# Two heads of a pair side by side on the halves of the matmul array

## Chip, core and metric

The kernel runs on one core of one Trainium2 chip. The metric is the device time of one execution in microseconds (us); less is better. TensorE (PE in the profile) does matmuls and transposes into PSUM, a small memory of eight banks per partition; VectorE (DVE), ScalarE (ACT) and GpSimd (POOL) do the elementwise work; SyncE (SP) issues the transfers. The array of TensorE is 128 rows (the contracted dimension) by 128 columns (the output partitions). A matmul whose contracted dimension is 64 uses one half of its rows, one whose output has 64 partitions one half of its columns; in the profile these have the forms 64\*128 and 128\*64.

## What is computed

An encoder of two layers on 1024 tokens of width 1024. Each layer projects x into the inputs of three groups, joins their outputs by one output projection, adds the residual and normalises, and then runs a gated feed-forward network with a second residual and norm. The groups are a gated linear recurrence, a retention with six heads of 64, and neighbourhood attention with four heads of 64 on a grid of 16 rows by 64 columns. Cut to the two groups at hand:

```
# retention, per head and chunk of 128 tokens
s = (q_chunk @ k_chunk.T) * decay          # 128 x 128
o = s @ v_chunk + (terms carried over the chunks), then a norm per head

# neighbourhood attention, per head: query (row, column) sees 8 x 16 keys
s = q @ k.T / 8 + bias(head, row distance, column distance)
p = softmax(s);  o = p @ v
```

## The kernel before

Activations are kept transposed (features on partitions, tokens along the free dimension). Heads come in pairs: a tile of 128 partitions holds head 0 in partitions 0 to 63 and head 1 in 64 to 127. Matmul operands of the large products are split into a high and a low part (`hi`, `lo`, type fp32r) and multiplied in three passes; the transposes and the products of attention values are plain fp32, where one matmul of the program appears as two instructions in the trace.

**Order of the work.** A layer is written as lists of steps that `weave` merges by their share of each list's cost, so that matmul-heavy steps (projections, output projection) stand between steps of the mixing groups. Below it the framework's list scheduler makes each engine's order at compile time: of what is ready it takes what stands first in the program, and it fills what it takes for a wait with later work. `order` fixes the order of two instructions of one engine. Buffers come from pools with tags: PSUM has `mm` (2 banks), `mx` (3, by `px_`), `mo` (1) and `ml` (2); SBUF has `T` (18 tiles of 4 KB per partition), `S` (8 of 2 KB), `Q` (4 of 2 KB) and others.

**Neighbourhood attention** (`na_mix`, L653) handles a pair of heads. A tile is 128 queries (8 rows by 16 columns: half `hf` of the rows, column block `cb`) of one head against 384 keys. Before, 16 tiles per pair run in the order head, half, column block, and a layer has two pairs, so 64 tiles in all. `scores` does two matmuls into one `mx` bank: the first contracts 128 rows (`nka` or `nkb`, which hold the high part of the keys in both halves, against the high and the low part of the head's queries), the second 64 rows (`nl`, the low part of the keys, in the head's own half). Then DVE adds the bias table and takes the maximum (L672), ACT makes the exponential and its sum (L675), DVE scales (L677). `values`, two tiles later in the list, transposes the three blocks of 128 keys into an `mx` bank (L691), ACT copies them (L693), and three fp32 matmuls of the form 128\*64 (six instructions) accumulate into the head's 64 partitions of `no`, the one `mo` bank. After the fourth column block ACT copies 64 partitions to `yna` (L702).

**Tables.** `na_table` (L636) builds the bias table of one head and half: one `T` tile (`tab`) and one `Q` tile (`tabc`), two POOL memsets (L641) and 16 transfers (L649, L650). Column blocks 0 to 2 read `tab`, block 3 reads `tabc`. With the head outermost, the query and key tiles of head 0 (`nqa`, `nka`) are last read half-way through a pair.

**What stands beside it.** The list of the layer's neighbourhood attention is woven with the projections of the second pair and the first half of the output projection (`wo`, tiles `res` of tag `T`), in one stage of about 126 us per layer.

**Retention** (`ret_mix`, `half`): per pair and half of the sequence, `scores` computes for each head four matmuls of the form 64\*128 into an `mx` bank, first all of head 0, then all of head 1, and DVE multiplies by the decay (L529). There are twelve such steps (two layers, three pairs, two halves), each of 16 instructions in the trace. The matmuls of `outs` (`o`) and of `kv` already alternate between the heads; those of `kv` are of the form 128\*64, as the values of neighbourhood attention are.

Of the kernel before, what the change touches and what calls it, by code (L numbers as in the profile page):

```python
# [11 lines left out]
AF = mybir.ActivationFunctionType  # L12
ALU = mybir.AluOpType
# [3 lines left out]
P = 128  # L17
# [13 lines left out]
TYPES = (0, 1, 1, 2)  # L31
# [21 lines left out]
class Trunk:  # L53
# [400 lines left out]
    def ret_mix(self, pr, z, ys):  # L454
        nc, l, V, A, G = self.nc, self.l, self.nc.vector, self.nc.scalar, self.nc.gpsimd
        blk = lambda t, w: t.rearrange("p (n i) -> p n i", i=w)
# [49 lines left out]
        def half(n4):  # L506
            sl = slice(n4 * 512, n4 * 512 + 512)
            w = {}

            def cross():  # L510
                w["qd"] = []
                for h in range(2):
                    hp = slice(h * 64, h * 64 + 64)
                    t = self.S("qd")
                    for d in range(2):
                        self.mark = G.tensor_tensor(out=blk(t, P)[d * 64 : d * 64 + 64, :, :], in0=blk(z["rq"][hp, sl], P),
                                                    in1=self.qw[hp, pr : pr + 1, d, :].to_broadcast([64, 4, P]), op=ALU.mult)
                    w["qd"].append(t)

            def scores():  # L520
                w["sd"] = []
                for h in range(2):
                    s = self.px_("s")
                    hp = slice(h * 64, h * 64 + 64)
                    for n in range(4):
                        c = (n4 * 4 + n) * P
                        self.mm(s[:, n * P : (n + 1) * P], z["rk"][hp, c : c + P], z["rq"][hp, c : c + P], True, True)
                    t = self.S("sd")
                    V.tensor_tensor(out=blk(t, P), in0=blk(s, P),  # L529
                                    in1=self.decay[:, 2 * pr + h : 2 * pr + h + 1, :].to_broadcast([P, 4, P]), op=ALU.mult)  # L530
                    w["sd"].append(t)

            def outs():
                o = self.px_("o")
                last = None
                for n in range(4):
                    m = n4 * 4 + n
                    c = slice(n * P, (n + 1) * P)
                    ks = slice(64 if m == 0 else 0, 64 if m == 7 else P)
                    ops = []  # L540
                    for h in range(2):
                        hp = slice(h * 64, h * 64 + 64)
                        ops.append((o[hp, c], z["st"][ks, m, hp], w["qd"][h][ks, c]))
                    for h in range(2):
                        hp = slice(h * 64, h * 64 + 64)
                        ops.append((o[hp, c], self.vc[pr][:, m, hp], w["sd"][h][:, c]))
                    for i, (out, lh, rh) in enumerate(ops):
                        ins = self.mm(out, lh, rh, i < 2, i >= 2)
                        if last is not None:
                            self.order(ins, last)  # L550
                        last = ins
                sq, sh, so = w["sd"][0], self.S("sqh", F32R), self.S("sql", F32R)
                A.activation(sh, o, AF.Square)
                A.activation(sq, o, AF.Square)
                self.lo(so, sq, sh)
                w["o"], w["sq"], w["sh"], w["sl"] = o, sq, sh, so

            def gnorm():
                sq = w["sq"]
                pv = self.px_("var")  # L560
                self.mm(pv, self.bones, w["sh"], True, False)
                self.mm(pv, self.bones, w["sl"], False, True)
                A.activation(sq, pv, AF.Ln, bias=self.gneps)
                A.activation(sq, sq, AF.Exp, scale=-0.5)
                V.tensor_tensor(out=sq, in0=w["o"], in1=sq, op=ALU.mult)
                V.scalar_tensor_tensor(out=ys[3 + pr][:, sl], in0=sq, scalar=self.gnw[:, l, pr : pr + 1], in1=z["sg"][:, sl],
                                       op0=ALU.mult, op1=ALU.mult)

            return [cross, scores, outs, gnorm]

        def spill():
# [79 lines left out]
        return tab[:, 0, :], tab[:, 1, :], tabc  # L651

    def na_mix(self, pr, z, ys):  # L653
        nc, V, A = self.nc, self.nc.vector, self.nc.scalar
        w = {}

        def scores(h, hf, cb):
            def step():
                if h == 0 and hf == 0 and cb == 0:
                    ys[6 + pr] = self.T("yna")  # L660
                if cb == 0:
                    w["tab"] = self.na_table(2 * pr + h, hf)
                grid = lambda t: t.rearrange("p (r c) -> p r c", c=64)
                hp = slice(h * 64, h * 64 + 64)
                s = self.px_("ns")
                c0 = COLS[cb]
                for i, (kp, b) in enumerate(((slice(0, P), z["nk"][h]), (hp, z["nl"]))):
                    self.mm(s[:, :384], z["nq"][h][kp, hf * 512 + cb * P : hf * 512 + cb * P + P],
                            grid(b)[kp, hf * 4 : hf * 4 + 12, c0 : c0 + 32], i == 0, i == 1)
                p = self.S("np")  # L670
                mx, sm = self.M("mx", 1), self.M("sm", 1)
                V.tensor_tensor_reduce(out=p[:, :384], in0=s[:, :384], in1=w["tab"][TYPES[cb]], scale=1.0,  # L672
                                       scalar=-3.0e38, op0=ALU.add, op1=ALU.max, accum_out=mx)
                V.tensor_scalar(mx, mx, -1.0, None, op0=ALU.mult)
                A.activation(p[:, :384], p[:, :384], AF.Exp, bias=mx, accum_out=sm)  # L675
                V.reciprocal(sm, sm)
                V.tensor_scalar(p[:, :384], p[:, :384], sm, None, op0=ALU.mult)  # L677
                w[h, hf, cb] = p

            return step  # L680

        def values(h, hf, cb):
            def step():
                hp = slice(h * 64, h * 64 + 64)
                if cb == 0:
                    w["o"] = self.ps("no", "mo")
                    w["last"] = None
                o, p = w["o"], w[h, hf, cb]
                pt = self.px_("npt")
                for g in range(3):  # L690
                    nc.tensor.transpose(pt[:, g * P : (g + 1) * P], p[:, g * P : (g + 1) * P], self.ident)  # L691
                pT = self.S("npT")
                A.activation(pT[:, :384], pt[:, :384], AF.Copy)  # L693
                for g in range(3):
                    gg = hf + g
                    ins = self.mm(o[hp, cb * P : (cb + 1) * P], self.vwin[gg][:, cb, (2 * pr + h) * 64 : (2 * pr + h) * 64 + 64],
                                  pT[:, g * P : (g + 1) * P], g == 0, g == 2)
                    if w["last"] is not None:
                        self.order(ins, w["last"])
                    w["last"] = ins  # L700
                if cb == 3:
                    A.activation(  # L702
                        ys[6 + pr][hp, hf * 512 : hf * 512 + 512].rearrange("p (r b c) -> p b r c", b=4, c=16)[:, :, :, ::-1],
                        o[hp, :].rearrange("p (b r c) -> p b r c", b=4, c=16), AF.Copy,
                    )

            return step

        tiles = [(h, hf, cb) for h in range(2) for hf in range(2) for cb in range(4)]
        steps = []  # L710
        for i in range(len(tiles) + 2):
            if i < len(tiles):
                steps.append(scores(*tiles[i]))
            if i >= 2:
                steps.append(values(*tiles[i - 2]))
        return steps


# [692 lines left out]
```

## Time and profile before

| | |
|---|---|
| time, median of 3 runs | 2349.53 us (2345.99 to 2353.46) |
| the profiled execution | 2347.68 us, span 2345.9 us |
| mean granted TensorE clock | 0.988 |
| TensorE busy | 2274.2 us, 97% |
| VectorE, ScalarE, GpSimd busy | 62%, 42%, 39% |

The span runs from the first to the last instruction. A matmul's shown duration includes its way through the array, so the durations of neighbours overlap; what a matmul costs TensorE is read from its start to the start of the next. PEld rows are loads of the stationary operand.

### The profile page before, as it was taken

The numbers are of one execution on the slowest core, as the hardware profiler recorded it, in microseconds if no ns is written. First come the engines' busy times: TensorE is split into PE (matmuls) and PEld (weight loads), VectorE is DVE, ScalarE is ACT, GpSimd is POOL, SyncE is SP. The second block draws the span as 40 slices with busy tenths as digits, with TensorE's granted clock in tenths as the row PEclk, the third lists the DMA queues.
The fourth block names the chain that finished last, engine by engine and source line by source line (L and its number), as shares of the span: only waits on it lengthen the run. The fifth ranks groups of instructions, "written<-read, shape, count | busy, mean of one in ns | idle before, by whom it ended". The sixth has DMA issues, their size and how long they took to land. (4 is left out here: it accounts for less than half of the span.)

```text
span 2345.9 us, 29309 instructions
## 1 busy us (share of the span) xinstructions
PE 2274.2 (97%) x10790; PEld 1834.5 (78%) x10790; DVE 1451.3 (62%) x2073; ACT 990.4 (42%) x1509; POOL 925.6 (39%) x568
## 2 busy tenths in 40 slices
PE   8999999999899999999989999999998999999998
PEld 6787777787678888888778878777876788888886
DVE  6966635578675656543658656455886656655336
ACT  5653345444233333443346533553542233344432
POOL 1424500054554343375513245000545543434655
PEclk9999999999999999999999999999999999999999
DMA  5232233424554445785321322333245444467852
GB/s 171 99 113 64 64 118 90 134 91 141 188 182 155 156 162 183 291 293 182 123 72 46 114 63 67 116 100 123 95 157 187 163 166 145 169 203 291 287 158 85
DMA packets 142696, 340.45 MB, mean 145 GB/s; under 512 B 24024, under 2 KB 37336, under 8 KB 142552
## 3 DMA queue, kind: packets, MB, share of 16 engines
q1 hardware_dynamic: 142552, 338.58, 43.7%
q8 instruction: 84, 1.38, 0.2%
q14 instruction: 60, 0.49, 0.1%
HBM read 242.88 MB, written 90.08 MB: 142 GB/s over the span
## 5 line engine op out<-in xcount | busy, mean ns | idle before, releaser
L116 PE MATMUL dn<-dw,hx 128*128 128x512 f32 x1848 | 422.0, 390 | 2.0 <-DVE rs L735 2.0
L116 PEld LDWEIGHTS dn<-dw,hx 128*128 128x128 f32 x1848 | 347.7, 188 | 74.5 <-DVE dw L122 2.4
L122 POOL TENSOR_TENSOR hx<-hraw,hx 128x1024 fp32r<-128x1024 f32 x80 | 207.7, 2611 | 195.3 <-ACT hx L119 188.5
L119 ACT ACTIVATE wsp<-qS 128x512 fp32r<-128x512 f32 x176 | 110.7, 631 | 277.5 <-PE w_up L116 134.6
L122 DVE TENSOR_TENSOR dw<-wraw,dw 128x1024 fp32r<-128x1024 f32 x84 | 124.4, 1488 | 158.0 <-ACT dw L119 147.8
L122 DVE TENSOR_TENSOR wsp<-qS,wsp 128x512 fp32r<-128x512 f32 x176 | 164.3, 935 | 62.9 <-ACT wsp L119 61.2
L119 ACT ACTIVATE dw<-wraw 128x1024 fp32r<-128x1024 f32 x84 | 83.1, 989 | 202.9 <-PE dn L116 187.3
L122 DVE TENSOR_TENSOR wl<-wraw,wh 128x1024 fp32r<-128x1024 f32 (+2 forms) x84 | 110.6, 1327 | 74.2 <-ACT wh L119 67.7
L119 ACT ACTIVATE wh<-wraw 128x1024 fp32r<-128x1024 f32 (+2 forms) x84 | 84.5, 1014 | 120.1 <-PE rg L116 27.6
L896 POOL TENSOR_TENSOR qS<-wraw 128x512 f32<-128x512 f32 x44 | 72.3, 1643 | 144.8 <-DVE wsp L122 75.1
L122 DVE TENSOR_TENSOR wsp<-wraw,wsp 128x512 fp32r<-128x512 f32 x100 | 114.4, 1147 | 23.8 <-ACT wsp L119 22.9
L119 ACT ACTIVATE wsp<-wraw 128x512 fp32r<-128x512 f32 x100 | 62.7, 629 | 130.5 <-PE w_up L116 76.4
L116 PE MATMUL wo<-wh,yh 128*128 128x512 f32 x256 | 104.1, 407 | 0.0
L116 PE MATMUL wo<-wl,yh 128*128 128x512 f32 x256 | 101.9, 398 | 0.0
L116 PE MATMUL wo<-wh,yl 128*128 128x512 f32 x256 | 100.9, 394 | 0.0
L1029 DVE TENSOR_TENSOR w_gate<-w_gate,w_gate 128x512 f32<-128x512 f32 x58 | 39.7, 684 | 90.2 <-PE w_gate L116 60.3
L119 ACT ACTIVATE hx<-hraw 128x1024 fp32r<-128x1024 f32 (+1 forms) x88 | 81.5, 940 | 18.2 <-DMA hraw<-hd 18.1
L116 PE MATMUL w_gate<-T1h,wsp 128*128 128x512 f32 x176 | 65.8, 438 | 18.2 <-DVE w_gate L1029 18.2
L896 POOL TENSOR_TENSOR qS<-qS,wraw 128x512 f32<-128x512 f32 x44 | 67.2, 1526 | 39.0 <-issue 32.6
L1011 POOL TENSOR_TENSOR qt<-wraw 128x512 f32<-128x512 f32 x22 | 29.0, 1319 | 134.8 <-issue 126.5
L896 POOL TENSOR_TENSOR qS<-wraw,wraw 128x512 f32<-128x512 f32 x44 | 60.2, 1369 | 55.4 <-DVE wsp L122 55.4
L395 POOL TENSOR_TENSOR tg<-tg,tg 128x1024 f32<-128x1024 f32 x6 | 16.0, 2673 | 162.5 <-DVE tg L381 87.5
(409 smaller groups left out, 6187.8 us busy)
## 6 DMA issues: line engine op xcount, KB each, us to landing
wraw<-in_w_down_dram SPq DMA_DIRECT2D x74, 512.0 KB
hraw<-hd SPq DMA_DIRECT2D x66, 512.0 KB
wraw<-in_w_gate_dram SPq DMA_DIRECT2D x52, 512.0 KB
wraw<-in_w_up_dram SPq DMA_DIRECT2D x52, 512.0 KB
wt<-qt SPq DMA_DIRECT2D x88, 256.0 KB
hd<-hid SPq DMA_DIRECT2D x80, 256.0 KB
wraw<-wt SPq DMA_DIRECT2D x40, 512.0 KB
wraw<-in_w_st_dram SPq DMA_DIRECT2D x36, 512.0 KB
```

What stands on the lines that cost most here:

```text
L116: return self.nc.tensor.matmul(out, lhsT=lhsT, rhs=rhs, start=start, stop=stop, skip_group_check=more)
L119: return self.nc.scalar.activation(out, src, AF.Copy, scale=scale)
L122: return (eng or self.nc.vector).tensor_tensor(out=out, in0=src, in1=hi.bitcast(F32), op=ALU.subtract)
L395: nc.gpsimd.tensor_tensor(out=y, in0=y, in1=yb, op=ALU.add)
L896: t = lambda o, x, y, op: eng.tensor_tensor(out=o, in0=x, in1=y, op=op)
L1011: t = lambda o, x, y: G.tensor_tensor(out=o, in0=x, in1=y, op=ALU.subtract)
L1029: add = lambda o, x, y: V.tensor_tensor(out=o, in0=x, in1=y, op=ALU.add)
```

## The change

In the retention's `scores` two `mx` banks are taken at once and the matmuls of the heads alternate. In `na_mix` a tile is now a pair: `scores(hf, cb)` takes two `mx` banks and issues the two matmuls over 128 rows (head 0, head 1) and then the two over 64 rows (head 0 in the lower, head 1 in the upper half); the softmax follows head by head. `values(hf, cb)` transposes both heads into `ml` banks, copies both, and issues the twelve instructions of the products with the heads alternating. The lookahead between scores and values is one step of two tiles where it was two steps of one. Two tables are built at once, eight steps stand where sixteen stood, and `yna` is copied for both heads in one ACT instruction.

```diff
@@ -519,14 +519,15 @@
 
             def scores():
                 w["sd"] = []
+                s = [self.px_("s") for _ in range(2)]
+                for n in range(4):
+                    for h in range(2):
+                        hp = slice(h * 64, h * 64 + 64)
+                        c = (n4 * 4 + n) * P
+                        self.mm(s[h][:, n * P : (n + 1) * P], z["rk"][hp, c : c + P], z["rq"][hp, c : c + P], True, True)
                 for h in range(2):
-                    s = self.px_("s")
-                    hp = slice(h * 64, h * 64 + 64)
-                    for n in range(4):
-                        c = (n4 * 4 + n) * P
-                        self.mm(s[:, n * P : (n + 1) * P], z["rk"][hp, c : c + P], z["rq"][hp, c : c + P], True, True)
                     t = self.S("sd")
-                    V.tensor_tensor(out=blk(t, P), in0=blk(s, P),
+                    V.tensor_tensor(out=blk(t, P), in0=blk(s[h], P),
                                     in1=self.decay[:, 2 * pr + h : 2 * pr + h + 1, :].to_broadcast([P, 4, P]), op=ALU.mult)
                     w["sd"].append(t)
 
@@ -651,68 +652,73 @@
         return tab[:, 0, :], tab[:, 1, :], tabc
 
     def na_mix(self, pr, z, ys):
+
         nc, V, A = self.nc, self.nc.vector, self.nc.scalar
         w = {}
-
-        def scores(h, hf, cb):
+        hp = slice(0, 64), slice(64, 128)
+        grid = lambda t: t.rearrange("p (r c) -> p r c", c=64)
+
+        def scores(hf, cb):
             def step():
-                if h == 0 and hf == 0 and cb == 0:
+                if hf == 0 and cb == 0:
                     ys[6 + pr] = self.T("yna")
                 if cb == 0:
-                    w["tab"] = self.na_table(2 * pr + h, hf)
-                grid = lambda t: t.rearrange("p (r c) -> p r c", c=64)
-                hp = slice(h * 64, h * 64 + 64)
-                s = self.px_("ns")
+                    w["tab"] = [self.na_table(2 * pr + h, hf) for h in range(2)]
                 c0 = COLS[cb]
-                for i, (kp, b) in enumerate(((slice(0, P), z["nk"][h]), (hp, z["nl"]))):
-                    self.mm(s[:, :384], z["nq"][h][kp, hf * 512 + cb * P : hf * 512 + cb * P + P],
-                            grid(b)[kp, hf * 4 : hf * 4 + 12, c0 : c0 + 32], i == 0, i == 1)
-                p = self.S("np")
-                mx, sm = self.M("mx", 1), self.M("sm", 1)
-                V.tensor_tensor_reduce(out=p[:, :384], in0=s[:, :384], in1=w["tab"][TYPES[cb]], scale=1.0,
-                                       scalar=-3.0e38, op0=ALU.add, op1=ALU.max, accum_out=mx)
-                V.tensor_scalar(mx, mx, -1.0, None, op0=ALU.mult)
-                A.activation(p[:, :384], p[:, :384], AF.Exp, bias=mx, accum_out=sm)
-                V.reciprocal(sm, sm)
-                V.tensor_scalar(p[:, :384], p[:, :384], sm, None, op0=ALU.mult)
-                w[h, hf, cb] = p
+                s = [self.px_("ns") for _ in range(2)]
+                for i in range(2):
+                    for h in range(2):
+                        kp, b = ((slice(0, P), z["nk"][h]), (hp[h], z["nl"]))[i]
+                        self.mm(s[h][:, :384], z["nq"][h][kp, hf * 512 + cb * P : hf * 512 + cb * P + P],
+                                grid(b)[kp, hf * 4 : hf * 4 + 12, c0 : c0 + 32], i == 0, i == 1)
+                for h in range(2):
+                    p = self.S("np")
+                    mx, sm = self.M("mx", 1), self.M("sm", 1)
+                    V.tensor_tensor_reduce(out=p[:, :384], in0=s[h][:, :384], in1=w["tab"][h][TYPES[cb]], scale=1.0,
+                                           scalar=-3.0e38, op0=ALU.add, op1=ALU.max, accum_out=mx)
+                    V.tensor_scalar(mx, mx, -1.0, None, op0=ALU.mult)
+                    A.activation(p[:, :384], p[:, :384], AF.Exp, bias=mx, accum_out=sm)
+                    V.reciprocal(sm, sm)
+                    V.tensor_scalar(p[:, :384], p[:, :384], sm, None, op0=ALU.mult)
+                    w[h, hf, cb] = p
 
             return step
 
-        def values(h, hf, cb):
+        def values(hf, cb):
             def step():
-                hp = slice(h * 64, h * 64 + 64)
                 if cb == 0:
                     w["o"] = self.ps("no", "mo")
                     w["last"] = None
-                o, p = w["o"], w[h, hf, cb]
-                pt = self.px_("npt")
+                o, pT = w["o"], []
+                for h in range(2):
+                    pt = self.ps("npt", "ml")
+                    for g in range(3):
+                        nc.tensor.transpose(pt[:, g * P : (g + 1) * P], w[h, hf, cb][:, g * P : (g + 1) * P], self.ident)
+                    pT.append(self.S("npT"))
+                    A.activation(pT[h][:, :384], pt[:, :384], AF.Copy)
                 for g in range(3):
-                    nc.tensor.transpose(pt[:, g * P : (g + 1) * P], p[:, g * P : (g + 1) * P], self.ident)
-                pT = self.S("npT")
-                A.activation(pT[:, :384], pt[:, :384], AF.Copy)
-                for g in range(3):
-                    gg = hf + g
-                    ins = self.mm(o[hp, cb * P : (cb + 1) * P], self.vwin[gg][:, cb, (2 * pr + h) * 64 : (2 * pr + h) * 64 + 64],
-                                  pT[:, g * P : (g + 1) * P], g == 0, g == 2)
-                    if w["last"] is not None:
-                        self.order(ins, w["last"])
-                    w["last"] = ins
+                    for h in range(2):
+                        ins = self.mm(o[hp[h], cb * P : (cb + 1) * P],
+                                      self.vwin[hf + g][:, cb, (2 * pr + h) * 64 : (2 * pr + h) * 64 + 64],
+                                      pT[h][:, g * P : (g + 1) * P], g == 0, g == 2)
+                        if w["last"] is not None:
+                            self.order(ins, w["last"])
+                        w["last"] = ins
                 if cb == 3:
                     A.activation(
-                        ys[6 + pr][hp, hf * 512 : hf * 512 + 512].rearrange("p (r b c) -> p b r c", b=4, c=16)[:, :, :, ::-1],
-                        o[hp, :].rearrange("p (b r c) -> p b r c", b=4, c=16), AF.Copy,
+                        ys[6 + pr][:, hf * 512 : hf * 512 + 512].rearrange("p (r b c) -> p b r c", b=4, c=16)[:, :, :, ::-1],
+                        o.rearrange("p (b r c) -> p b r c", b=4, c=16), AF.Copy,
                     )
 
             return step
 
-        tiles = [(h, hf, cb) for h in range(2) for hf in range(2) for cb in range(4)]
+        tiles = [(hf, cb) for hf in range(2) for cb in range(4)]
         steps = []
-        for i in range(len(tiles) + 2):
+        for i in range(len(tiles) + 1):
             if i < len(tiles):
                 steps.append(scores(*tiles[i]))
-            if i >= 2:
-                steps.append(values(*tiles[i - 2]))
+            if i >= 1:
+                steps.append(values(*tiles[i - 1]))
         return steps
```

## Rows read from the trace of the kernel before

**Rows 1.** The page, part 1: busy time of each engine.
```profile
PE 2274.2 (97%) x10790; PEld 1834.5 (78%) x10790; DVE 1451.3 (62%) x2073; ACT 990.4 (42%) x1509; POOL 925.6 (39%) x568
```

**Rows 2.** Busy time by stretch: the neighbourhood stage of each layer (stretch, then length).
```profile
337.60:464.00 126.40, 126.22 (x619) 89.78 (x618) 69.76 (x206) 61.03 (x138) 6.09 (x10) 1.00 0.37 107
1509.00:1637.00 128.00, 127.82 (x633) 91.71 (x632) 69.08 (x200) 60.38 (x136) 6.09 (x10) 1.00 0.39 117
```

**Rows 3.** Timeline of TensorE in the first stage: start, length, instruction, count.
```profile
377.03 0.44 PE L116 MATMUL ns<-nl,nqb 64*128 64x384 f32 x1
377.40 0.50 PE L116 MATMUL wo<-wh,yh 128*128 128x512 f32 x1
377.74 0.39 PE L116 MATMUL wo<-wh,yl 128*128 128x512 f32 x1
377.97 0.40 PE L116 MATMUL wo<-wl,yh 128*128 128x512 f32 x1
378.30 0.87 PE L116 MATMUL no<-npT,vwin 128*64 128x128 f32 x6
379.10 0.33 PE L691 MATMUL npt<-ident,np 128*128 128x128 f32 x1
```

**Rows 4.** Timeline of TensorE, scores behind an output-projection matmul.
```profile
385.36 0.34 PE L116 MATMUL ns<-nkb,nqb 128*128 128x384 f32 x1
385.62 0.44 PE L116 MATMUL ns<-nl,nqb 64*128 64x384 f32 x1
386.00 0.55 PE L691 MATMUL npt<-ident,np 128*128 128x128 f32 x3
386.30 0.42 PE L116 MATMUL ns<-nkb,nqb 128*128 128x384 f32 x1
```

**Rows 5.** Timeline of TensorE, a `kv` step of the retention.
```profile
177.40 1.09 PE L116 MATMUL kv<-vw,kT 128*64 128x128 f32 x16 [1.75 <-POOL vw L473]
178.43 0.50 PE L116 MATMUL rq<-xh,wh 128*128 128x512 f32 x1
```

**Rows 6.** Instructions of tile `kv`: duration in ns, least, median, most.
```profile
L116 PEld LDWEIGHTS kv<-vw,kT x192: 132/137/137, 177.4 to 1454.7; 128*64 128x64 f32 x192
```

**Rows 7.** Timeline of TensorE, two places of the retention's scores.
```profile
191.01 1.71 PE L116 MATMUL s<-rq,rk 64*128 64x128 f32 x16
192.65 0.50 PE L116 MATMUL rk<-xh,wl 128*128 128x512 f32 x1
...
209.03 1.16 PE L116 MATMUL s<-rq,rk 64*128 64x128 f32 x8
210.12 0.51 PE L116 MATMUL rg<-xl,wh 128*128 128x512 f32 x1
```

**Rows 8.** Groups of instructions, whole span: count, busy us, mean ns, idle before.
```profile
L116 PE MATMUL no<-npT,vwin 128*64 128x128 f32 x384 | 55.6, 281 | 0.4
```

**Rows 9.** The same by form, first neighbourhood stage alone.
```profile
L675 ACT ACTIVATE np<-np,mx 128x384 f32<-128x384 f32 x32 | 19.5, 610 | 9.7 <-DVE mx L674 9.6
L693 ACT ACTIVATE npT<-npt 128x384 f32<-128x384 f32 x32 | 15.2, 487 | 33.2 <-PE npt L691 33.0
L677 DVE TENSOR_SCALAR np<-np,sm 128x384 f32<-128x384 f32 x32 | 14.0, 440 | 0.6
L672 DVE CUSTOM_DVE_ANT_0 np<-ns,tab 128x384 f32<-128x384 f32 x24 | 13.2, 551 | 12.5 <-PE ns L116 9.4 <-DMA tabc<-ubias 3.0
L641 POOL MEMSET tab<- 128x768 f32 x6 | 4.4, 736 | 39.8 <-DMA tabc<-ubias 18.5 <-PE ns L116 12.0 <-DVE mx L672 9.3
```

**Rows 10.** SP in the first stage: a stretch of its timeline, then a wait.
```profile
356.75 7.38 SPq L649 DMA_DIRECT2D tab<-ubias  x16
...
SPq L649 <- POOL tab L641: 15.0, 3, 12.4
```

**Rows 11.** Waits of TensorE, whole span: total us, times, longest.
```profile
PE w_gate L116 <- DVE w_gate L1029: 18.2, 6, 3.6
```

**Rows 12.** Busy time by stretch, the first stage and what follows it.
```profile
337.60:597.00 259.40, 258.15 (x1231) 197.81 (x1229) 178.66 (x377) 120.61 (x237) 71.97 (x56) 1.00 0.38 120
```

## Prediction

> **What bounds the kernel now.** I read four views, in this order. The page's first part says that TensorE is busy 97% of the span and the next engine, VectorE, 62% [rows 1]. An average can hide a stage with another limit, so the second view is the busy time of the two stretches in which neighbourhood attention runs: TensorE is busy 126.2 of 126.4 us and 127.8 of 128.0 us there, VectorE 55% and ScalarE 48%, at full granted clock [rows 2]. The third is the waits: over the whole span TensorE's largest is behind these stages, 18.2 us in six pieces for VectorE in the gate product [rows 11], and in the two stretches the view lists no wait of TensorE at all. So a microsecond of TensorE work that goes from there shortens the kernel by one, unless something behind TensorE becomes the limit. The fourth is the timeline, read from start to start, since busy can also mean that the array waits for itself. There the price of small matmuls shows:
>
> Two output-projection matmuls of 512 columns start 0.23 us apart; the one before six `no` instructions holds TensorE 0.33 us (377.97 to 378.30): entering the half-column form costs 0.10. The six take 0.80 (378.30 to 379.10) [rows 3]. The matmul behind a half-array run is stretched too: 0.34 for 0.23 (377.40 to 377.74), 0.11 more [rows 3]; where a short transpose follows there is less to stretch, so I take 0.08 for leaving.
>
> A `ns` matmul over 128 rows holds 0.26 before the switch to the half-row form (385.36 to 385.62); by the pace of 0.23 for 512 columns its 384 columns need 0.17, so 0.09 is the switch. The 64-row matmul then holds 0.38 (385.62 to 386.00, and 0.37 at 377.03) [rows 3, 4], that is 0.17 of columns and 0.2 of exposed load and switch back.
>
> **Part 1, the values.** A tile of one head costs 0.10 + 0.80 + 0.08 = 0.98. What two heads in turn cost is on show in `kv`, which has the same form and already alternates: 16 instructions hold 1.03 us (177.40 to 178.43) [rows 5]. Six instructions of `no` on one half take 0.80, so eight on one half would take at most 0.80 x 8/6 = 1.07, while `kv` puts sixteen into that time: the second half is free. Twelve `no` instructions in turn should hold what six hold now, 0.80. Each pair of tiles saves one tile's 0.98; there are 32 pairs (384 instructions of `no`, six to a tile [rows 8]): **31.4 us**. Their order is fixed by `order`, so no scheduler can undo it.
>
> The Trainium skill ("TensorE: Matmul & The Clock Gate", Part 3) says that a weight load overlaps running matmuls only where the row group differs; both heads of the values use all rows. By that rule each load of 0.137 us would stand in line, and the sixteen of `kv` would take 2.2 us at least [rows 6]; the row shows 1.03, so the trace disagrees and the sum goes by the row. By the rule the pairing would save only switches, which is the fourth rival below.
>
> **Part 2, the scores.** A tile costs 0.26 + 0.38 + 0.08 = 0.72 and two cost 1.44. A pair: 0.17 for head 0 over 128 rows, 0.26 for head 1, then both 64-row matmuls, 0.38 if they run side by side plus 0.01, then 0.08: 0.90. That saves 0.54, in 32 pairs **17.3 us**. The trace has no two fp32r matmuls side by side on row halves. Upper end: free, as said. Lower end: one behind the other, 0.17 more, 0.37 saved and 11.8 us in all. I take the upper end, because the nearest row, the retention's scores, has the same 64\*128 form and shows overlap where the heads meet: 16 instructions that begin as head 0 and go on as head 1 hold 1.64 [rows 7], less than two separate eights at 1.09 each.
>
> The Trainium skill (same page, Part 3) gives the span of matmuls packed on row groups as one duration plus about 4 ns for each further one. By it the pair costs 0.90 and the sum stays 17.3; no row here shows it at the full fp32r pace.
>
> **Part 3, the retention's scores.** Eight of the twelve steps read like the first of [rows 7], 1.64 us. Paired, they should cost what `kv`'s sixteen do, 1.03, plus 0.05 for a load of 128 instead of 64 columns at the start: 1.08. Saved: 8 x 0.56 = **4.5 us**. In the other four the heads stand apart, 1.09 each and other matmuls between (209.03 is such a second half), because a third `mx` bank was not free. There the change finds the same bank missing; it saves between nothing and 1.3 each (2 x 1.09 + 0.2 for a second entry - 1.08). I take a quarter of 5.2: **1.3 us**.
>
> **What costs nothing.** Fewer and larger `yna` copies, transposes in `ml` banks and two tables at a time leave the work of ScalarE, VectorE, GpSimd and SP the same. In a stage of 104 us VectorE would be at 67% and ScalarE at 58%; TensorE's projections and output projection cover the softmax. Its chain for a pair is 2 x (0.55 + 0.61 + 0.44) = 3.2 [rows 9], some 3.6 with the small instructions between, and a pair stands every 104/16 = 6.5 us. Without that cover a pair would cost 3.6 where TensorE needs some 2.5 (0.80 + 0.18 + 0.90 + six transposes, 0.6).
>
> **What is taken back.** A `scores` step needs two of three `mx` banks, so a step that comes early finds one; its heads go apart and save nothing. I take 3 of 16 in each layer: 6 x 0.54 = 3.2 us. At the end of each stage the last step has one more head to transpose and copy before its values (0.3 for three transposes [rows 4], 0.49 for the copy [rows 9]): 0.8, twice, 1.6 us; output-projection matmuls may hide it, I charge it.
>
> **Sum.** 31.4 + 17.3 + 4.5 + 1.3 - 3.2 - 1.6 = 49.7 us. The profiled execution took 2347.68 us, which gives 2298; it lies 1.85 below the median of the runs, so the forecast is **2300 us**. With all four split steps won and nothing taken back it is 58.4 us and 2291; leaving at 0.11 instead of 0.08 adds 32 x 2 x 0.03 = 1.9, and the gate's waits of 18.2 [rows 11] may move by a few us either way with the new schedule, so the low end is 2285.
>
> **The rivals.**
>
> *Tables come late.* Head 0's query and key tiles now live until the pair's end, and two tables of `T` are in use where one was, in a pool of 18 that also feeds `res`. If a set of two can't be begun before the old one is free, it costs two memsets of 0.74 and two smaller ones, some 2.4 [rows 9], and 32 issues on SP at 7.38/16 = 0.46, 14.8 [rows 10]: 17.2 us. Three sets a layer in full view make the stage 16 x 3.6 + 3 x 17.2 = 109 instead of 104 us: 10 us lost in both layers, 2310. For it: SP already waits up to 12.4 us for a table's memset [rows 10]. Against: column block 3 reads `tabc`, so `tab` comes free a step early, and TensorE has projections to do meanwhile.
>
> *The same, and it decides: slower than before.* A stage as long as now needs (126 - 58)/3 = 23 us a set. With the 12.4 us wait added to the 17.2, a set takes 29.6 and the stage 146: 20 us more in each layer, less 5.8 from the retention: 2384. It needs every set to be built wholly in series, which the rows don't show.
>
> *Scores don't overlap, or are taken apart throughout.* The 64-row matmuls run one behind the other: 5.5 us less, 2306; if the scheduler separates all pairs, 14 less, 2314.
>
> *The change doesn't do what it says:* halves in turn run one behind the other in the values as well. Then only switches are saved: 2 x 0.98 - (0.18 + 0.80 + 6 x 0.11) = 0.3 in the values, 0.37 in the scores, 32 of each, some 22 us: 2328. `kv` speaks against it.
>
> *It is given back behind the stage.* From the first stage's start to the gate's waits VectorE is busy 178.7 of 259.4 us [rows 12], 109 of them in the 133 us behind the stage, or 82%. If half of the 44 us from the two stages turns into more waits of the gate for VectorE (18.2 now), the time is 2322. Against: that work hangs on the output projection's tiles and moves forward with them.
>
> **How the numbers follow.** Chances: forecast 0.66; late tables 0.11; scores apart 0.08; no overlap at all 0.03; given back 0.06; slower by tables or another disorder of the schedule 0.05; gains and losses about even 0.01. The range takes in all cases up to giving back, and a little for their own spread: **2285 to 2324**. About 0.3%, 7 us, is what a measurement of this kernel can tell from no change. Faster 0.93, same 0.02, slower 0.05.
>
> **What would show it.** Right: `no` in runs of twelve that hold about 0.8 us with pair partners starting within 0.01; 64-row `ns` matmuls of two heads starting together and holding 0.38; both neighbourhood stages near 104 us with TensorE without waits; the retention's scores at 1.1 us. Wrong: a TensorE wait for VectorE at L672 or the table's transfers, runs of `ns` with one head alone, 64-row partners 0.17 apart, or more than 18 us of gate waits.

## The result and the profile after

The changed kernel takes 2321.25 us in the median (2320.11 to 2325.28), the kernel before 2351.49 beside it: a ratio of 0.9877 with a 95% interval of 0.9858 to 0.9896, so 29 us less (24 to 33). The forecast was 2300, 50 us less, with a range of 2285 to 2324. The sign is right and the time lies in the range, near its upper end; a good 20 us of the forecast gain did not come.

The busy times of the page's first part answer to [rows 1]:

```profile
PE 2241.5 (97%) x10790; PEld 1811.2 (78%) x10790; DVE 1444.5 (62%) x2073; ACT 983.9 (42%) x1501; POOL 920.7 (40%) x568
```

TensorE's busy time fell by 33 us and the other engines have the work they had, as they should. Where it fell is best read over a stretch that holds the same instructions in both kernels: from the first `ns` matmul of a layer to the last `wo` (848 instructions on TensorE). Busy time by stretch of the kernel before, one row for each layer (stretch, length, then PE, PEld, DVE, ACT, POOL, clock, DMA):

```profile
337.70:511.83 174.13, 173.95 (x848) 129.37 (x847) 102.96 (x270) 80.44 (x164) 35.74 (x31) 1.00 0.34 105
1506.20:1680.33 174.13, 173.95 (x848) 129.38 (x847) 102.97 (x270) 80.44 (x164) 35.74 (x31) 1.00 0.33 105
```

The same stretches of the changed kernel:

```profile
334.16:495.98 161.82, 161.01 (x848) 121.32 (x847) 102.65 (x270) 77.59 (x159) 35.15 (x30) 1.00 0.35 113
1491.40:1652.98 161.58, 161.02 (x848) 121.32 (x847) 102.70 (x270) 77.80 (x159) 35.07 (x30) 1.00 0.34 113
```

Each is 12.3 and 12.6 us shorter, where the forecast's terms for this stage, 31.4 + 17.3 - 3.2 - 1.6, say 22 each. TensorE is still busy for all but 0.8 us of the first and 0.6 of the second: it is not idle, it does something that the sum left out. The waits of TensorE agree; these are the one behind the stage, which answers to [rows 11], and the largest that is new in it:

```profile
PE w_gate L116 <- DVE w_gate L1035: 17.3, 6, 3.6
```

```profile
PE no L116 <- ACT npT L698: 1.2, 4, 0.4
```

The timeline of TensorE in the changed kernel shows what happened, in four places (start, length, instruction, count): the retention's sixteen, twelve `no`, values taken apart with the scores around them, and four scores that stayed together.

```profile
191.93 1.16 PE L116 MATMUL s<-rq,rk 64*128 64x128 f32 x16
193.02 0.50 PE L116 MATMUL rk<-xh,wl 128*128 128x512 f32 x1
...
342.29 0.88 PE L116 MATMUL no<-npT,vwin 128*64 128x128 f32 x12
343.10 0.50 PE L116 MATMUL nk<-xl,wh 128*128 128x512 f32 x1
...
347.67 0.42 PE L116 MATMUL ns<-nka,nqa 128*128 128x384 f32 x1
347.93 0.34 PE L116 MATMUL ns<-nkb,nqb 128*128 128x384 f32 x1
348.32 0.43 PE L116 MATMUL no<-npT,vwin 128*64 128x128 f32 x2
348.68 0.44 PE L116 MATMUL ns<-nl,nqa 64*128 64x384 f32 x1
349.05 0.87 PE L116 MATMUL no<-npT,vwin 128*64 128x128 f32 x10
349.85 0.44 PE L116 MATMUL ns<-nl,nqb 64*128 64x384 f32 x1
...
365.03 0.34 PE L116 MATMUL ns<-nka,nqa 128*128 128x384 f32 x1
365.21 0.34 PE L116 MATMUL ns<-nkb,nqb 128*128 128x384 f32 x1
365.48 0.44 PE L116 MATMUL ns<-nl,nqa 64*128 64x384 f32 x1
365.48 0.44 PE L116 MATMUL ns<-nl,nqb 64*128 64x384 f32 x1
365.85 0.50 PE L116 MATMUL wo<-wh,yh 128*128 128x512 f32 x1
```

Twelve `no` hold 0.81 us (342.29 to 343.10; forecast 0.80). Four `ns` hold 0.82 before leaving (365.03 to 365.85, as forecast: 0.17 + 0.26 + 0.39), and the two 64-row matmuls start together. The retention's sixteen hold 1.09 (forecast 1.08). But the third block shows what most values do: the first two `no` instructions go alone, then other work (here a 64-row matmul of the scores), then the other ten. Counted over the trace, 28 of the 32 pairs of values run as 2 and 10, four as 12. Of the 32 pairs of scores twelve keep their four matmuls together; six are cut by `no` as in the third block, two by transposes, and in twelve the heads go one after the other, most with other work between them.

### The profile page after: what moved, and what is told of

It is laid out like the page before. It is cut to its first block, busy times and chain, and to the rows that moved or that the text cites. A ratio compares the mean times of both kernels' runs of the same rounds, so it can differ in the third digit from the quotient of the medians.

```text
span 2318.3 us, 29337 instructions
## 1 busy us (share of the span) xinstructions
PE 2241.5 (97%) x10790; PEld 1811.2 (78%) x10790; DVE 1444.5 (62%) x2073; ACT 983.9 (42%) x1501; POOL 920.7 (40%) x568
## 5 line engine op out<-in xcount | busy, mean ns | idle before, releaser
L902 POOL TENSOR_TENSOR qS<-wraw 128x512 f32<-128x512 f32 x44 | 65.0, 1477 | 142.6 <-DVE wsp L122 74.0
L642 POOL MEMSET tab<- 128x768 f32 x16 | 12.7, 794 | 182.0 <-DMA vd<-nv 46.9
L116 PE MATMUL w_gate<-T1h,wsp 128*128 128x512 f32 x176 | 64.5, 431 | 20.6 <-DVE w_gate L1035 17.3
```

Source lines behind the costliest of these rows:

```text
L116: return self.nc.tensor.matmul(out, lhsT=lhsT, rhs=rhs, start=start, stop=stop, skip_group_check=more)
L642: self.order(nc.gpsimd.memset(t, NEG), self.mark)
L902: t = lambda o, x, y, op: eng.tensor_tensor(out=o, in0=x, in1=y, op=op)
```

## Experiments

All ratios below are to the kernel before, run beside each.

**1. Twelve instructions that become ready together.** The products begin with the head that ScalarE copies last:

```diff
                 for g in range(3):
-                    for h in range(2):
+                    for h in (1, 0):
                         ins = self.mm(o[hp[h], cb * P : (cb + 1) * P],
```

> The changed kernel with one edit: the products of the values begin with head 1, whose transposed scores are copied last, so that all twelve instructions become ready together. Theory A (the gain was lost because the first two instructions of a pair's values go alone as soon as head 0 is copied, and open and close the half-array form once more): no more runs of 2 and 10; 32 runs of 12 at 0.81 us where 28 pairs now cost 0.36 + 0.80 and one more entry and exit of about 0.18, so 28 x 0.54 = 15 us less, near 2306, and somewhat less again if the scores' four matmuls stay together more often. Theory B (the split only filled time in which TensorE would otherwise wait for the second copy of 0.49 us, or the stage has another limit): runs of 12, but new waits of TensorE for the copy, and the time stays within 5 us of 2321.

Measured: 2312.99 us, ratio 0.9837 (0.9817 to 0.9857). TensorE's timeline, the busy times over the two stretches from first `ns` to last `wo`, TensorE's wait for the copies over the whole span, and the second layer's retention, from its first `kv` to the first `ns`:

```profile
347.35 0.42 PE L116 MATMUL ns<-nka,nqa 128*128 128x384 f32 x1
347.61 0.34 PE L116 MATMUL ns<-nkb,nqb 128*128 128x384 f32 x1
347.88 0.44 PE L116 MATMUL ns<-nl,nqa 64*128 64x384 f32 x1
347.88 0.44 PE L116 MATMUL ns<-nl,nqb 64*128 64x384 f32 x1
...
348.51 0.88 PE L116 MATMUL no<-npT,vwin 128*64 128x128 f32 x12
```

```profile
333.83:489.15 155.32, 154.00 (x849) 118.42 (x847) 103.12 (x270) 77.51 (x160) 34.91 (x30) 1.00 0.38 118
1489.88:1644.65 154.77, 153.52 (x848) 118.43 (x847) 103.05 (x270) 77.51 (x159) 34.80 (x30) 1.00 0.37 118
```

```profile
PE no L116 <- ACT npT L698: 2.1, 4, 0.8
```

```profile
1326.91:1489.88 162.97, 155.47 (x995) 127.35 (x996) 87.33 (x131) 66.36 (x105) 57.12 (x44) 0.97 0.25 76
```

All 32 pairs run as twelve, and the scores of the next pair, which had been cut by the first two `no`, stay whole in the same place; eighteen pairs of scores are whole now instead of twelve. The stretches lose 6.5 and 6.8 us more, 13.3 of the 15 that theory A names. Theory B fails: the scheduler had other work for the time of the second copy, and TensorE's wait for it is 2.1 us in all, after 1.2 in the changed kernel. The time itself fell by 8, 0.4 points of the ratio, and the two intervals just don't overlap. In the profiled execution the span fell by 5 (2318.3 to 2313.3), since the second layer's retention took 162.97 us where the changed kernel's takes 157.24 (1334.16 to 1491.40). The edit touches no step of that stage. Up to 3 us of the difference can be the clock, granted at 0.97 there where the changed kernel has 0.99, so more of the stage ran at the lower level of 1.2 GHz (an estimate, 2% of 163 us); experiment 5 comes to that stage.

**2. Scores that are tied together.** On top of 1, an order among the four matmuls:

```diff
+                s, last = [self.px_("ns") for _ in range(2)], None
 ...
-                        self.mm(s[h][:, :384], ...)
+                        ins = self.mm(s[h][:, :384], ...)
+                        if last is not None:
+                            self.order(ins, last)
+                        last = ins
```

> The values' products begin with head 1 as in h1_first, and the scores' four matmuls are ordered (head 0 and head 1 over 128 rows, then head 0 and head 1 over 64), so that the 64-row matmuls of a pair always stand together, while a first 128-row matmul may stand alone. Theory A (the rest of the missing gain lies in pairs of scores that the list scheduler takes apart, some 14 of 32, each worth 0.4 to 0.5 us): 5 to 8 us below h1_first's 2313, so 2305 to 2308. Rival (the pairs stand apart because the second mx bank is late, and tying them makes TensorE wait for it or delays head 0's softmax): waits of TensorE at the ns rows, no gain or a loss, 2313 or more.

Measured: 2306.68 us, ratio 0.9814 (0.9796 to 0.9832), the lowest median of all, though the interval overlaps with that of experiment 1. Busy time over the two stretches, and TensorE's largest wait in the stage:

```profile
335.02:488.57 153.55, 151.25 (x848) 117.36 (x847) 102.69 (x270) 77.59 (x160) 34.98 (x30) 1.00 0.38 119
1483.82:1637.19 153.37, 151.08 (x849) 117.36 (x847) 102.68 (x270) 77.60 (x159) 34.80 (x30) 1.00 0.38 119
```

```profile
PE no L116 <- ACT npT L701: 2.4, 2, 1.2
```

The 64-row matmuls now stand in pairs everywhere; the stretches lose 1.8 and 1.4 us more, 3 together. TensorE's busy time there falls by 5.2, as expected, but it waits more: 2.3 us of each stretch are not busy, after 1.3. So the time came out as theory A says partly by luck: 3 of the 6 us between the medians are the ties', and the profiled execution also has a quicker retention in the second layer, 155.71 us (1328.11 to 1483.82) at the full clock, where experiment 1's had 162.97 at 0.97. With both edits the stretches are 20.6 and 20.8 us shorter than before, against the 22 forecast for each.

**3. Each pairing undone.** In the changed kernel the scores, or the values, head by head:

```diff
-                for i in range(2):
-                    for h in range(2):
+                for h in range(2):
+                    for i in range(2):
                         kp, b = ((slice(0, P), z["nk"][h]), (hp[h], z["nl"]))[i]
```

> The changed kernel with the scores' four matmuls head by head (128 rows and 64 rows of head 0, then of head 1), all else as changed. Theory A (pairing the 64-row matmuls saves 0.17 plus two switches, some 0.5 us, where the four stay together, which the changed kernel does in about 12 to 20 of 32 pairs): 5 to 9 us more than the changed kernel, 2326 to 2330. Theory B (row halves at the fp32r pace don't really run side by side): within 3 us of 2321.

Measured: 2329.31 us, ratio 0.991 (0.9893 to 0.9927), within what theory A gives. The stretches:

```profile
334.71:500.17 165.46, 164.78 (x849) 122.72 (x848) 103.32 (x270) 77.51 (x160) 34.90 (x30) 1.00 0.35 110
1496.85:1661.57 164.72, 164.71 (x848) 122.72 (x847) 102.69 (x270) 77.65 (x160) 35.01 (x30) 1.00 0.35 111
```

They are 3.6 and 3.1 us longer than in the changed kernel: pairing the row halves pays, and in the kernel as changed it brings 7 us.

```diff
-                for g in range(3):
-                    for h in range(2):
+                for h in range(2):
+                    for g in range(3):
                         ins = self.mm(o[hp[h], cb * P : (cb + 1) * P],
```

> The changed kernel with the values' products head by head (six instructions of head 0, then six of head 1), all else as changed. Theory A: where the twelve stand together they cost 1.45 and one entry and exit, where they are taken apart 2 x 0.98; 18 of the first kind and 14 of the second are 57 us against 46 now: some 10 us more than the changed kernel, near 2331. Theory B (the column halves bring nothing, the switches alone do): within 4 us of 2321.

Measured: 2325.25 us, ratio 0.9891 (0.987 to 0.991). The stretches, and two places where the twelve stand together:

```profile
333.52:496.10 162.58, 162.46 (x848) 125.36 (x847) 103.21 (x270) 77.69 (x160) 34.97 (x30) 1.00 0.36 112
1491.06:1653.61 162.55, 162.44 (x849) 125.37 (x847) 103.15 (x270) 77.73 (x160) 34.90 (x30) 1.00 0.36 112
```

```profile
347.94 1.25 PE L116 MATMUL no<-npT,vwin 128*64 128x128 f32 x12
349.11 0.44 PE L116 MATMUL ns<-nl,nqa 64*128 64x384 f32 x1
349.12 0.44 PE L116 MATMUL ns<-nl,nqb 64*128 64x384 f32 x1
...
354.42 1.15 PE L116 MATMUL no<-npT,vwin 128*64 128x128 f32 x12
355.49 0.50 PE L116 MATMUL nq<-xh,wh 128*128 128x512 f32 x1
```

Only 0.8 and 1.0 us longer than in the changed kernel, and the time lies between the two theories. The counts were as expected: 18 pairs stand as twelve and 14 as six and six, none as 2 and 10. Two other things were wrong in the expectation of 10. Twelve in series don't hold the 1.45 of two serial sixes but 1.07 us in twelve places (354.42 to 355.49) and 1.17 in six (347.94 to 349.11): some of the second head's instructions ran beside the first head's. And the scores gain: where `no` had cut them, both 64-row matmuls now go together (349.11 and 349.12). Counted from start to start, the values hold 42.4 us here and 35.8 in the changed kernel, 6.6 more; the scores hold 35.2 and 38.1, 2.9 less; and the half-column form is entered 46 times instead of 60, which is 2.5 less at 0.18 each. These add up to 1.2 of the 1.7 us measured. So in the kernel as changed, alternating the values brought about 2 us in all: what the halves side by side saved, the extra entries and the cut scores took.

**4. Fewer tables.** All heads and halves of a layer use the first pair of tables:

```diff
-                    w["tab"] = [self.na_table(2 * pr + h, hf) for h in range(2)]
+                    if pr == 0 and hf == 0:
+                        self.tabs = [self.na_table(2 * pr + h, hf) for h in range(2)]
+                    w["tab"] = self.tabs
```

> The changed kernel with two of the sixteen bias tables built in each pass over the layer's first half and used for all heads and halves of the layer; it leaves out 12 of 16 table builds (24 memsets and 192 transfers), so its output is not the reference's. Rival theory (tables come late and hold up the neighbourhood stage): 5 to 10 us less than the changed kernel's 2321. Theory A (TensorE is never without work in the stage): within 4 us of 2321.

This leaves out 12 of the 16 tables and so computes something else. Measured: 2324.94 us, ratio 0.9885 (0.9864 to 0.9906), no faster than the changed kernel. The stretches are 160.50 us each, 1.3 and 1.1 less than with all tables:

```profile
335.72:496.22 160.50, 160.33 (x849) 120.77 (x847) 101.04 (x270) 77.55 (x159) 29.68 (x21) 1.00 0.28 99
1495.18:1655.68 160.50, 160.33 (x848) 120.77 (x847) 101.13 (x270) 77.54 (x160) 29.70 (x21) 1.00 0.29 99
```

So late tables account for 2.4 us at most; they are not where the gain went.

**5. The retention's part.** Alone on the kernel before, and left out of the changed kernel and of experiment 2:

```diff
+                s = [self.px_("s") for _ in range(2)]
+                for n in range(4):
+                    for h in range(2):
 ...
                 for h in range(2):
-                    s = self.px_("s")
```

> The kernel before with the retention's scores alternating and nothing else. If what TensorE saves there shortens the kernel: eight of twelve steps from 1.64 to 1.09, 4.4 us less than before, near 2346. If the steps behind wait for VectorE and ScalarE as long as before, the gain is given back in the second layer as it seems to be in the changed kernel: within 2 us of before.

Measured: 2350.61 us, ratio 0.9994 (0.9981 to 1.0008): no change that can be told. Yet `s` holds 1.09 us in the same eight places. Busy time of its retention stages, from first `kv` to first `ns`, and of two pieces of the second:

```profile
177.43:333.25 155.82, 151.63 (x995) 124.04 (x996) 85.23 (x131) 66.31 (x105) 58.19 (x42) 0.99 0.27 78
1345.55:1506.42 160.87, 153.88 (x995) 125.71 (x996) 86.97 (x131) 66.32 (x105) 56.34 (x42) 0.98 0.25 75
...
1360.00:1380.00 20.00, 16.18 (x101) 12.47 (x98) 18.17 (x24) 6.75 (x10) 11.86 (x8) 0.99 0.32 87
1380.00:1400.00 20.00, 20.00 (x119) 15.41 (x119) 9.79 (x10) 9.23 (x14) 9.07 (x7) 0.92 0.08 27
```

The kernel before, in the same stages:

```profile
177.40:337.70 160.30, 154.46 (x995) 126.63 (x996) 88.49 (x131) 66.34 (x105) 56.34 (x42) 0.99 0.26 76
1349.48:1506.20 156.72, 152.97 (x995) 125.66 (x996) 87.20 (x131) 66.35 (x105) 56.96 (x42) 1.00 0.26 78
```

In the profiled execution the first stage is 4.5 us shorter and the second 4.2 longer. There the granted clock is 0.98 of the full 2.4 GHz, and 0.92 in the second piece, so a part of it ran at the lower level of 1.2; in the 20 us ahead of that piece TensorE had been without work for 3.8. The row of the kernel before has 1.00 for the whole stage.

> The changed kernel with the retention's scores as they were before (all of head 0, then all of head 1). If the retention's part brings nothing by itself because the steps behind it wait for VectorE and ScalarE, and the granted clock falls in the second layer where it did not: within 3 us of the changed kernel's 2321. If it brings what TensorE saves there: 5 us more, 2326.

Measured: 2328.55 us, ratio 0.9898 (0.9879 to 0.9916), where the changed kernel has 0.9877.

> As scores_tied, with the retention's scores as before. It shows whether the two parts add: if the retention's part brings nothing, the same time as scores_tied within 3 us; if the retention's alternation costs something in the second layer through waits and the granted clock, a few us less than scores_tied; if it brings 5 us, 5 more.

Measured: 2312.86 us, ratio 0.9831 (0.9812 to 0.9849), where experiment 2 has 0.9814, in runs beside it. Both retention stages together, sums of the same view, for the changed kernel and for the same without the retention's part:

```profile
sum 313.12, PE 304.04 PEld 248.80 DVE 169.31 ACT 132.62 POOL 116.43; mean PE 152.02 PEld 124.40 DVE 84.65 ACT 66.31 POOL 58.22
sum 318.64, PE 309.01 PEld 253.61 DVE 174.23 ACT 132.59 POOL 115.26; mean PE 154.51 PEld 126.80 DVE 87.11 ACT 66.30 POOL 57.63
```

Beside the kernel before, the retention's part brings nothing (316.69 us in the two stages after 317.02). Beside the attention's it seems to bring 4 to 5 us by the ratios, with intervals that overlap, and in the stages of one profiled execution each 5.5 us, and 4.8 beside experiment 2 (318.60 against 313.75). What can be said is that it saves TensorE 0.55 us in each of eight places and that the stage, which also waits for other engines and at times runs at the lower clock, passes on between none of it and all. Why it passes on less beside the kernel before stays open; the lower clock in its second layer can be a part of it (up to 3 us of 161, an estimate from the granted 0.98 and 1.00 in the two rows).

## Why the prediction came out as it did

**The prices held.** The durations of the three new runs came out as forecast: 0.81 for twelve alternating values (0.80), 0.82 for four scores (0.82), 1.09 for the retention (1.08). TensorE was the limit of the neighbourhood stage and stayed it, and what was taken from it there came off the end: by experiment 2 the two stretches are 41.3 us shorter than before and the span 41.7 (2345.9 to 2304.2). The 64-row matmuls, which no row of before showed at this pace, start together and hold 0.37 (365.48 to 365.85) like one alone in [rows 3]; there the trace agrees with the Trainium skill ("TensorE: Matmul & The Clock Gate", Part 3), whose span for packed row groups is one duration and some nanoseconds. The rule of the Trainium skill, in the same place, that loads overlap only where the row group differs is contradicted once more: with all weight loads of both heads in the same rows, twelve `no` hold 0.81, where twelve loads of 0.137 [rows 6] in line would take 1.6.

**The step that failed** is the end of part 1: "Their order is fixed by `order`, so no scheduler can undo it." An order fixes what comes before what, not that nothing comes between. Head 0's copy is done some 0.5 us before head 1's, so its first matmul, two instructions, was ready alone and stood first in the program; the scheduler issued it, filled the wait with other work and came back for ten. That is 0.36 us (348.32 to 348.68) and another entry and exit of 0.18, while the ten still hold 0.80 like twelve, since one half has its six to do anyway: 0.54 in 28 pairs, 15 us of the 31.4. Experiment 1 shows it: 13.3 us in the two stretches from the order of two heads alone, a part of it from scores that became whole.

**A term that was too small** is the 3.2 us for scores taken apart, 3 of 16 in each layer, so 6 of 32. In the changed kernel 20 of 32 were apart. In six of them the early `no` and its ten fell between, and experiment 1 made these whole; fourteen are still apart there, and the ties of experiment 2 brought 3 us more. The forecast's reason, the second `mx` bank, may hold for those, since in experiment 2 a first 128-row matmul still stands alone in fourteen pairs; no run tests it.

**The retention**, 5.8 us, was forecast as if its stage were bound by TensorE as the other is. The busy times of [rows 2] were read for the neighbourhood stages alone; the same view of the retention's, shown in experiment 5, has TensorE without work for 5.8 of 160.3 us and 3.8 of 156.7, and what is saved there is not passed on with certainty.

**The rivals.** Late tables are worth 2.4 us at most by experiment 4. The gate's waits are 17.3 us after 18.2 [rows 11], so nothing was given back behind the stage. "Scores taken apart" came true in part; that the values would be taken apart was not among the rivals, and it was the largest loss. Of the retention's twelve steps four still stand apart, so the 1.3 us hoped for from them did not come.

That the time still lies in the range is luck: its upper end was set by gains given back behind the stage, which did not happen, and covered a loss that nobody had in view.

With both edits 43.7 us (1 - 0.9814) of the forecast 49.7 are there.

## What to carry to other kernels

The price of a half-array run lies in its entry and exit, 0.18 us here where one pair of instructions takes 0.11; so two heads side by side pay in full only where the scheduler keeps the run whole. Begin such a run with the operand that is ready last, and read the order of instructions, not the list of steps: a chain of order edges does not keep other work out. And ask of each stage whether it is bound by the engine that is relieved; in the bound stage here nearly all of the saving came through, in the other between none and all.

## What the runs showed of the hardware

Two fp32r matmuls of 384 columns on the two row halves start within 0.01 us and hold 0.37 together, as one does, each into 128 partitions of its own PSUM bank. And instructions of the other half overlap even when they don't alternate: twelve values in series hold 1.07 to 1.17 us, where two sixes without a switch between them would hold 1.46 (0.80 and 6 x 0.11), and the kernel before holds 1.64 for sixteen scores in series [rows 7] where the alternating sixteen hold 1.09. In the trace of the values in series the second head's first instruction starts 0.28 us after the first head's (341.93 and 341.66), before the first head's six are through; of the orders tried, only alternating reaches 0.81.
